# Turning an FFN's activations by 32x32 blocks and a trip through DRAM instead of TensorE transposes, with the down product one group later

## The chip, the cores and the metric

One core of a Trainium2 chip runs the whole program. The metric is the device time of one execution in microseconds. "Before" is the kernel without the change; three runs of it were timed and one execution was profiled.

## What is computed

Two blocks of a transformer, 256 tokens of width 1024, batch 1, float32 throughout. The first block has two layers, each FFN, mixer, FFN, with a gMLP mixer in the first layer and latent attention (MLA) in the second; the second block has retention and forgetting attention side by side and one more FFN. So there are five FFNs, and they are all this:

```python
def swiglu(n, w_gate, w_up, w_down):
    return (jax.nn.silu(n @ w_gate) * (n @ w_up)) @ w_down

f = swiglu(rms_norm(h, ffn_pre_g[layer, 0]), ffn_w_gate[layer, 0], ffn_w_up[layer, 0], ffn_w_down[layer, 0])
h = h + 0.5 * rms_norm(f, ffn_post_g[layer, 0])
```

The hidden width is 2816 = 11 x 256 in all five.

## The kernel before

**Tokens and weights.** The 256 tokens are two streams of 128 rows. Weights arrive from DRAM as chunks of 128x1024 floats, in the order of use, through SyncE's queue (`fetch`, line 153: the load at 158, three `raw` buffers). Each chunk is split into a rounded part `hi` (ScalarE cast, line 337) and the rest `lo` (VectorE subtract, line 338), in a ring of nine. A product of float32 accuracy is three matmuls, hi x hi, hi x lo, lo x hi (`mm3`, lines 166 to 169). A chunk costs each stream six matmuls of 512 columns. Stream 0 uses chunk s when stream 1 uses chunk s - 5, so two streams share each chunk while it is in the ring. The main loop (line 1134) takes one step a chunk; `later(st, n, fn, ...)` (line 192) runs `fn` when n + 1 more chunks of that stream are done.

**An FFN.** `ffn` (line 357) goes over 11 groups (NG) of 256 hidden columns. `up(j)` takes four chunks and makes gate and up of the group in one PSUM tile `g` of 128x512; ScalarE and VectorE make f = silu(gate) x up from it, 128 tokens by 256 columns (lines 364 to 367). The down product needs f with hidden columns on the partitions. Two chunks after, `turn(j)` (line 372) transposes the two halves of f on TensorE into PSUM, with an identity, and splits the result into `fth` and `ftl`. `down(j)` takes two chunks, 12 matmuls, and adds to the accumulator `a`. The loop at line 391 puts `down(j - 1)` after `up(j)`; the last two groups of the last FFN are held to the end:

```python
        for j in range(NG):
            yield from up(j)
            if 0 < j < NG - 2 * last:
                yield from down(j - 1)
```

`phases` (line 1211) lists the chunks in the same order, `layout` (line 1150) puts the weights into that form on the host.

**Between parts.** When a part of a stream ends, `post` (line 280) makes the next input x: ScalarE squares the accumulator, VectorE adds the two sums (line 295), GpSimd takes the power (`pow_`, line 143), VectorE makes x with it (line 299), and TensorE transposes x (line 217, `tr<-cst,x`). `prepare` (line 261) brings the gain rows `pg` and `gn` through SyncE's queue during an FFN; a small GpSimd copy into each (`touch`, line 196) sets the moment.

The order of the instructions on each engine is set by a scheduler from the program's order and its priorities; TensorE, VectorE, ScalarE, GpSimd and SyncE each work their own list in order.

Of the kernel before, what the change touches and what calls it, by code (L numbers as in the profile page):

```python
# [9 lines left out]
F32 = mybir.dt.float32  # L10
F32R = mybir.dt.float32r
# [5 lines left out]
P = 128  # L17
D = 1024
KD = D // P
FF = 2816  # L20
NG = FF // 256
# [88 lines left out]
def body(ctx: ExitStack, tc: tile.TileContext, a: dict, out: bass.AP, stop=None, dbg=None):  # L110
    nc = tc.nc
    V, S, G, PE = nc.vector, nc.scalar, nc.gpsimd, nc.tensor

    base = ctx.enter_context(tc.tile_pool(name="base", bufs=1))
    ring = ctx.enter_context(tc.tile_pool(name="ring", bufs=1))
    psg = ctx.enter_context(tc.tile_pool(name="psg", bufs=2, space=bass.MemoryType.PSUM))
    psa = ctx.enter_context(tc.tile_pool(name="psa", bufs=1, space=bass.MemoryType.PSUM))
    pst = ctx.enter_context(tc.tile_pool(name="pst", bufs=2, space=bass.MemoryType.PSUM))

    def f32(x):  # L120
        return x.bitcast(F32)
# [70 lines left out]
    def later(st, n, fn, *args):  # L192

        st.later.append([n + 1, fn, args])
# [128 lines left out]
    def acc_tile(st):  # L323
        return [psa.tile([P, 512], F32, name=f"a{st.t}{q}") for q in range(2)]

    def g_tile():
        return psg.tile([P, 512], F32, name="g")
# [8 lines left out]
    def split(hi, lo, src):  # L336
        S.copy(hi, src)  # L337
        V.tensor_tensor(lo, src, f32(hi), op=ALU.subtract)  # L338
# [6 lines left out]
    def unit(st, ps, lhs=None, nq=4, nk=2, n=512):  # L345

        for q in range(nq):
            w = yield
            k_gemm(ps, lhs or st.xt, w, nk * q, q == 0, q == nq - 1, nk, n)
# [7 lines left out]
    def ffn(st, inner={}, last=False):  # L357
        fts = {}

        def up(j):  # L360
            ps = g_tile()
            yield from unit(st, ps)
            th = base.tile([P, 256], F32, name="th", tag="th", bufs=2)
            S.activation(th, ps[:, :256], AF.Tanh, scale=st.ch)  # L364
            V.scalar_tensor_tensor(th, th, 1.0, ps[:, :256], op0=ALU.add, op1=ALU.mult)  # L365
            f = base.tile([P, 256], F32, name="f", tag="f", bufs=2)
            V.scalar_tensor_tensor(f, th, st.cc, ps[:, 256:], op0=ALU.mult, op1=ALU.mult)  # L367
            fts[j] = f
            st.mark = f[:, 0:1]
            later(st, 2, turn, j)  # L370

        def turn(j):
            f = fts[j]
            tr = pst.tile([P, 4, P], F32, name="tr")
            for k in range(2):
                PE.transpose(tr[:, k, :], f[:, k * P:(k + 1) * P], ident)  # L376
            pool, n = (enter("last"), 6) if last and j > 5 else (base, 3)
            hi = pool.tile([P, 2, P], F32R, name="fth", tag="fth", bufs=n)
            lo = pool.tile([P, 2, P], F32R, name="ftl", tag="ftl", bufs=n)
            split(hi, lo, tr[:, :2, :])  # L380
            fts[j] = hi, lo

        def down(j):
            if j == 0:
                st.acc = acc_tile(st)
            for k in range(2):
                w = yield
                f = fts[j]
                rows_gemm(st.acc, f, w, k, j + k == 0, j == NG - 1 and k == 1)

        for j in range(NG):
            yield from up(j)
            if 0 < j < NG - 2 * last:
                yield from down(j - 1)
            if callable(inner.get(j)):
                inner[j]()
            elif j in inner:
                yield from inner[j]
        for j in range(NG - 1 - 2 * last, NG):
            yield from down(j)  # L400


    def gmlp(st, pool):
# [352 lines left out]
    def block2(st, pool):  # L756
# [168 lines left out]
        ps = yield from next_unit()  # L925
        vr = pool.tile([P, 512], F32, name="vr", tag="vr", bufs=1)
        S.activation(vr, ps, AF.Copy, scale=st.c)
        orr = pool.tile([P, 512], F32, name="orr", tag="orr", bufs=2)
        sT = pool.tile([P, 4, P], F32, name="sT", tag="sT", bufs=1)

        def retain():
# [68 lines left out]
        for q in range(2):  # L1000
            tr = transposes(st, m[q], 0)
# [5 lines left out]
        with urgent():  # L1007
            for q in range(2):
                c = slice(512 * q, 512 * q + 512)
# [5 lines left out]
    def enter(name):  # L1015
        if name not in pools:
            pools[name] = [tc.alloc_tile_pool(name=name, bufs=1), 0]
        return pools[name][0]
# [92 lines left out]
    n = len(chunks)  # L1111
# [38 lines left out]
def layout(i):  # L1150

    c = np.ascontiguousarray
    o = {}

    def cols(w, unit, nk=2):

        k, n = w.shape
        return c(w.reshape(k // (P * nk), nk, P, n // unit, unit).transpose(3, 0, 2, 1, 4)).reshape(-1, P, nk * unit)

    def rowsw(w):  # L1160

        return w.reshape(-1, P, w.shape[1])

    def gu(g, u):
        both = np.stack([g.reshape(D, NG, 256), u.reshape(D, NG, 256)], 2).reshape(D, NG * 512)
        return cols(both, 512)

    fl = [(i["ffn_w_gate"][l, k], i["ffn_w_up"][l, k], i["ffn_w_down"][l, k]) for l in range(2) for k in range(2)]
    fl.append((i["w_gate_2"][0], i["w_up_2"][0], i["w_down_2"][0]))
    for n, (g, u, d) in enumerate(fl):  # L1170
        o[f"gu{n}"] = gu(g, u)
        o[f"dn{n}"] = rowsw(d)
    o["win"] = cols(i["gmlp_w_in"][0], 512)
    o["wgo"] = rowsw(i["gmlp_w_out"][0])
    o["wdq"] = cols(i["mla_w_dq"][0], 512)
    o["wdkv"] = cols(i["w_dkv"], 320)
    uq = i["mla_w_uq"][0].reshape(512, NH, 192)
    o["wuqr"] = cols(c(uq[:, :, P:]).reshape(512, 512), 512)
    o["wuq"] = cols(c(uq[:, [0, 2, 4, 6, 1, 3, 5, 7], :P]).reshape(512, 1024), 512)
    ukv = i["w_ukv"].reshape(256, NH, 256)  # L1180
    o["wukv"] = np.concatenate([cols(c(ukv[:, :, k * P:(k + 1) * P]).reshape(256, 1024), 512) for k in range(2)])
    wo = i["mla_w_o"][0].reshape(NH, P, D)
    o["wo"] = c(wo[[0, 2, 4, 6, 1, 3, 5, 7]])
    w2 = i["w_in_2"][0]
    big = np.concatenate([w2[:, 1536:2048], w2[:, 2048:2560], w2[:, 2560:3072], w2[:, 0:512], w2[:, 512:1024],
                          w2[:, 1024:1536], w2[:, 3080:4104], w2[:, 4104:5128]], 1)
    o["w2"] = cols(big, 512)
    o["w2f"] = c(w2[:, 3072:3080].reshape(8, P, 8).transpose(1, 0, 2)).reshape(P, 64)
    o["wro"] = rowsw(i["w_ret_o_2"][0])
    o["wfo"] = rowsw(i["w_fox_o_2"][0])  # L1190
    o["wout"] = rowsw(i["w_out_2"][0])
    gl = [i["ffn_pre_g"][0, 0], i["ffn_pre_g"][0, 1], i["ffn_pre_g"][1, 0], i["ffn_pre_g"][1, 1], i["mix_pre_g"][0],
          i["mix_pre_g"][1], i["kv_norm_g"], i["kv_a_norm_g"], i["mla_q_norm_g"][0], i["g_mix_2"][0], i["g_ffn_2"][0], i["g_ret_norm_2"][0],
          np.concatenate([i["g_fox_q_2"][0]] * 2), np.concatenate([i["g_fox_k_2"][0]] * 2)]
    o["pre"] = np.stack([gl[k] for k in (4, 1, 2, 5, 3, 9)])
    o["kva"], o["qn"] = i["kv_a_norm_g"].reshape(1, 256), i["mla_q_norm_g"].reshape(1, 512)
    o["gains"] = c(np.concatenate([g.reshape(-1, P).T for g in gl], 1))
    o["ffn_post_g"] = c(i["ffn_post_g"].reshape(4, D))
    o["mix_post_g"] = c(i["mix_post_g"])
    o["gmlp_ln_g"] = c(i["gmlp_ln_g"])  # L1200
    o["gmlp_ln_b"] = c(i["gmlp_ln_b"])
    o["b_forget_2"] = c(i["b_forget_2"])
    o["ws"] = c(i["gmlp_w_s"][0].transpose(2, 0, 1)).reshape(P, 16 * P)
    o["bs"] = c(i["gmlp_b_s"][0].T)
    o["x"] = c(i["x"][0])
    o["positions"] = c(i["positions"].reshape(2, P).T)
    o["c1"], o["c2"] = constants()
    return o


def phases(aps):
    def ch(name, idx):
        w = aps[name]
        return w[idx], w.shape[-1]

    def run(name, first, n):
        return [ch(name, k) for k in range(first, first + n)]

    def ffn(n, inner={}, last=False):
        r = []  # L1220
        for j in range(NG):
            r += run(f"gu{n}", 4 * j, 4)
            if 0 < j < NG - 2 * last:
                r += run(f"dn{n}", 2 * j - 2, 2)
            r += inner.get(j, [])
        return r + run(f"dn{n}", 2 * (NG - 1 - 2 * last), 2 + 4 * last)

    gm = run("win", 16, 16)
    for j in range(4):
        gm += run("win", 4 * j, 4)  # L1230
        if j:
            gm += run("wgo", 4 * j - 4, 4)
    gm += run("wgo", 12, 4)
    ml = run("wdq", 0, 4) + run("wukv", 0, 4) + run("wuqr", 0, 2) + run("wuq", 0, 4) + run("wo", 0, 8)
    b2 = run("w2", 0, 24)
    b2 += run("w2", 24, 8) + run("wro", 0, 4)
    b2 += run("w2", 32, 8) + run("wfo", 0, 4)
    b2 += run("wout", 0, 8)
    return [ffn(0), gm, ffn(1), ffn(2, {2: run("wdkv", 0, 4)}), ml, ffn(3), b2, ffn(4, last=True)]
# [18 lines left out]
```

## Time and profile before

| | |
|---|---|
| median of 3 runs | 1398.04 us (1396.69 to 1398.93) |
| the profiled execution | 1396.79 us, of which 1394.9 us are the trace's span |
| TensorE busy, matmuls | 1376.0 us, 99% |
| VectorE busy | 957.0 us, 69% |
| ScalarE busy | 717.2 us, 51% |
| GpSimd busy | 59.7 us, 4% |
| DMA engines, mean busy share of the main queue | 57.7%, 182 GB/s |

Matmuls are pipelined and their ends are modelled, so 99% says that TensorE is hardly ever without a matmul, not that it is at its peak. The weight loads of TensorE (81%) overlap the matmuls. Rows of the trace give the line of the kernel, the tile written and the tiles read, and in brackets the idle time before with what ended it.

### The profile page before, as it was taken

What the parts mean: (1) busy time and instruction counts of PE and PEld (TensorE: products, weight loads), DVE (VectorE), ACT (ScalarE), POOL (GpSimd) and SP (SyncE); (2) the same over time, 40 slices, a digit from 0 to 9 for tenths busy, and PEclk for the clock granted to TensorE, in tenths of its full rate; (3) what the DMA queues carried; (4) which work ended last, traced back from release to release, by engine and by line L of the source; (5) the groups of instructions that cost most, each with busy time, mean ns of one, the idle gap of its engine ahead of it and who ended that gap; (6) DMA issues with size and microseconds to landing.
All of it is one profiled execution on the core that took longest, in us unless ns stands there. A gap on an engine that the chain in (4) does not pass through costs nothing.

```text
span 1394.9 us, 17750 instructions
## 1 busy us (share of the span) xinstructions
PE 1376.0 (99%) x6402; PEld 1125.1 (81%) x6402; DVE 957.0 (69%) x1530; ACT 717.2 (51%) x1043; POOL 59.7 (4%) x81
## 2 busy tenths in 40 slices
PE   8999999999999999999999999999999999999998
PEld 5888887887788887888877888888878788888887
DVE  7775579977757558775569676665677865765554
ACT  6644456555544445544456655444567544544442
POOL 0000020000000001000001010000020000000000
PEclk9999999999999999999999999999999999999999
DMA  7666667554566664666655336666544355565662
GB/s 250 201 220 185 188 250 222 157 191 151 181 191 217 186 192 143 201 220 195 188 190 179 124 130 183 202 201 191 199 137 150 119 168 183 171 190 185 192 185 88
DMA packets 71656, 254.45 MB, mean 182 GB/s; under 512 B 8592, under 2 KB 10000, under 8 KB 71184
## 3 DMA queue, kind: packets, MB, share of 16 engines
q1 hardware_dynamic: 70992, 252.78, 57.7%
q8 instruction: 51, 0.84, 0.2%
q10 hardware_dynamic: 576, 0.52, 0.1%
q14 instruction: 37, 0.30, 0.1%
HBM read 252.23 MB, written 1.05 MB: 182 GB/s over the span
## 4 chain that ended last, share of the span: by engine, by line
PE 87%; DVE 6%; ACT 2%; DMA 2%; issue 1%; POOL 1%; SPq 0%; DVEq 0%; ACTq 0%; POOLq 0%
PE g L167 16%; PE g L168 16%; PE g L169 16%; PE a L169 11%; PE a L167 11%; PE a L168 11%; DVE lo L338 2%; PE tr L376 2%; PE tr L217 2%; DMA raw<-in_win 1%; POOL sm L145 1%; ACT hi L337 1%; DMA raw<-in_gu 1%; PE tr L459 0%; PE tr L722 0%
## 5 line engine op out<-in xcount | busy, mean ns | idle before, releaser
L338 DVE TENSOR_TENSOR lo<-raw,hi 128x1024 fp32r<-128x1024 f32 (+2 forms) x462 | 560.8, 1216 | 307.2 <-ACT hi L337 305.6
L337 ACT CAST hi<-raw 128x1024 fp32r<-128x1024 f32 (+2 forms) x462 | 481.2, 1044 | 428.8 <-PE g L169 205.7
L167 PE MATMUL g<-hi,xth 128*128 128x512 f32 x1040 | 414.3, 398 | 2.2 <-ACT hi L337 1.8
L168 PE MATMUL g<-lo,xth 128*128 128x512 f32 x1040 | 407.6, 392 | 2.0 <-DVE lo L338 2.0
L169 PE MATMUL g<-hi,xtl 128*128 128x512 f32 x1040 | 406.3, 391 | 0.0
L167 PEld LDWEIGHTS g<-hi,xth 128*128 128x128 f32 x1040 | 195.4, 188 | 43.0 <-ACT hi L337 3.5
L169 PEld LDWEIGHTS g<-hi,xtl 128*128 128x128 f32 x1040 | 195.4, 188 | 41.3 <-DVE sm L255 0.2
L168 PEld LDWEIGHTS g<-lo,xth 128*128 128x128 f32 x1040 | 195.6, 188 | 41.0 <-DVE lo L338 3.7
L167 PE MATMUL a<-hi,fth 128*128 128x512 f32 x440 | 175.7, 400 | 0.0
L168 PE MATMUL a<-lo,fth 128*128 128x512 f32 x440 | 172.0, 391 | 0.0
L169 PE MATMUL a<-hi,ftl 128*128 128x512 f32 x440 | 171.9, 391 | 0.0
L169 PEld LDWEIGHTS a<-hi,ftl 128*128 128x128 f32 x440 | 82.6, 188 | 17.4
L364 ACT ACTIVATE th<-g,ch 128x256 f32<-128x256 f32 x110 | 52.3, 475 | 86.4 <-PE g L169 85.2
L168 PEld LDWEIGHTS a<-lo,fth 128*128 128x128 f32 x440 | 82.8, 188 | 15.5
L167 PEld LDWEIGHTS a<-hi,fth 128*128 128x128 f32 x440 | 82.6, 188 | 15.5
L167 PE MATMUL a<-hi,xth 128*128 128x512 f32 x232 | 94.0, 406 | 0.7 <-ACT xth L337 0.6
L168 PE MATMUL a<-lo,xth 128*128 128x512 f32 x232 | 91.0, 394 | 0.0
L169 PE MATMUL a<-hi,xtl 128*128 128x512 f32 x232 | 90.9, 395 | 0.0
L365 DVE SCALAR_TENSOR_TENSOR th<-th,g 128x256 f32<-128x256 f32 x110 | 45.9, 418 | 43.5 <-ACT th L364 43.4
L337 ACT CAST fth<-tr 128x256 fp32r<-128x256 f32 x110 | 40.5, 369 | 37.6 <-PE tr L376 37.6
L367 DVE SCALAR_TENSOR_TENSOR f<-th,cc,g 128x256 f32<-128x256 f32 x110 | 52.8, 480 | 3.5
L167 PEld LDWEIGHTS a<-hi,xth 128*128 128x128 f32 x232 | 43.6, 188 | 10.3 <-ACT xth L337 2.1
(318 smaller groups left out, 1187.0 us busy)
## 6 DMA issues: line engine op xcount, KB each, us to landing
raw<-in_gu SPq DMA_DIRECT2D x220, 512.0 KB, 3.6
raw<-in_dn SPq DMA_DIRECT2D x110, 512.0 KB, 3.9
raw<-in_w SPq DMA_DIRECT2D x40, 512.0 KB, 3.3
raw<-in_win SPq DMA_DIRECT2D x32, 512.0 KB, 4.3
raw<-in_wgo SPq DMA_DIRECT2D x16, 512.0 KB, 3.6
raw<-in_wo SPq DMA_DIRECT2D x8, 512.0 KB, 3.3
raw<-in_wout SPq DMA_DIRECT2D x8, 512.0 KB, 3.3
gn<-in_pre SPq DMA_DIRECT2D x6, 512.0 KB, 5.3
```

The lines of the kernel that those rows point to most:

```text
L145: G.tensor_tensor(o, i, hp if up else hn[:, :n], op=ALU.pow)
L167: PE.matmul(o, l[0], r[0], start=start, stop=False)
L168: PE.matmul(o, l[0], r[1], start=False, stop=False)
L169: PE.matmul(o, l[1], r[0], start=False, stop=stop_)
L217: PE.transpose(tr[:, k, :], src[:, (4 * ngroup + k) * P:(4 * ngroup + k + 1) * P], ident)
L337: S.copy(hi, src)
L338: V.tensor_tensor(lo, src, f32(hi), op=ALU.subtract)
L364: S.activation(th, ps[:, :256], AF.Tanh, scale=st.ch)
L365: V.scalar_tensor_tensor(th, th, 1.0, ps[:, :256], op0=ALU.add, op1=ALU.mult)
L367: V.scalar_tensor_tensor(f, th, st.cc, ps[:, 256:], op0=ALU.mult, op1=ALU.mult)
L376: PE.transpose(tr[:, k, :], f[:, k * P:(k + 1) * P], ident)
```

## The change

In groups 0 to 7 of the first four FFNs and 0 to 9 of the last, f no longer goes through TensorE. VectorE transposes it by 32x32 blocks into `ft`; a DMA from GpSimd's queue writes `ft` to a DRAM tile `far`; four chunks later four DMAs of the same queue read `far` back into `fr` in the order in which blocks stand in their places, with a fixed permutation of the hidden columns that is made good in the rows of the down weights (`layout`). One chunk later `fr` is split into `fth` and `ftl` as `tr` was. The other groups are turned as before. `fr` has one buffer for both streams; `ft` shares the two buffers of `th`. `down(j)` follows `up(j + 2)` instead of `up(j + 1)`, and the FFN's last products are gathered at its end as the table `downs` says. To make room, one tile of the second block (`orr`) has one buffer in place of two.

```diff
-            later(st, 2, turn, j)
+            if j > (9 if last else 7):
+                later(st, 2, turn, j)
+                return
+
+            ft = base.tile([P, 256], F32, name="ft", tag="th", bufs=2)
+            V.transpose(ft, f)
+            far = dram.tile([4, 32, 4, 64], F32, name="far", bufs=6)
+            nc.gpsimd.dma_start(far.rearrange("a i c r -> (a i) (c r)"), ft)
+            later(st, 4, back, j, far)
+
+        def back(j, far):
+            fr = base.tile([P, 4, 64], F32, name="fr", bufs=1)
+            for c in range(4):
+                nc.gpsimd.dma_start(fr[32 * c:32 * c + 32], far[:, :, c, :].rearrange("a i r -> i a r"))
+            later(st, 1, parts, j, fr.rearrange("p a (k i) -> p k a i", k=2))
...
+        def parts(j, fr):
+            f = fts[j] = f_tiles(j)
+            split(*(x.rearrange("p k (a i) -> p k a i", a=4) for x in f), fr)
...
             yield from up(j)
-            if 0 < j < NG - 2 * last:
-                yield from down(j - 1)
+            for k in downs(j, last):
+                yield from down(k)
...
-        orr = pool.tile([P, 512], F32, name="orr", tag="orr", bufs=2)
+        orr = pool.tile([P, 512], F32, name="orr", tag="orr", bufs=1)
...
+        k = 10 if n == 4 else 8
+        d = d.reshape(NG, 4, 2, 32, D)
+        o[f"dn{n}"] = np.concatenate([d[:k].transpose(0, 2, 1, 3, 4).reshape(-1, P, D), d[k:].reshape(-1, P, D)])
...
+def downs(j, last):
+
+    if last:
+        return [j - 2] if 2 <= j < 9 else [7, 8, 9, 10] if j == 10 else []
+    return {0: [], 1: [], 9: [7, 8], 10: [9, 10]}.get(j, [j - 2])
```

How it moves instructions is best seen in three places. The first is TensorE in the first FFN, where the down products of the two streams meet (`a` are the accumulators, `g` the up products, `tr` the transposed f, `cst` the identity). Before:

```order
L167 MATMUL a_456<-hi,fth 128x512
L168 MATMUL a_456<-lo,fth 128x512
L169 MATMUL a_456<-hi,ftl 128x512
L376 MATMUL tr<-cst,f 128x128 x2
L167 MATMUL a_331<-hi,fth 128x512
L168 MATMUL a_331<-lo,fth 128x512
L169 MATMUL a_331<-hi,ftl 128x512
L167 MATMUL a_332<-hi,fth 128x512
L168 MATMUL a_332<-lo,fth 128x512
L169 MATMUL a_332<-hi,ftl 128x512
L376 MATMUL tr<-cst,f 128x128 x2
L167 MATMUL g<-hi,xth_225 128x512
```

The two pairs of transposes, one for each stream's f, stand among the matmuls of the weights in every group; with the change they stand there only in groups 8 to 10 (group 10 in the last FFN), and nothing takes their place.

The second is GpSimd in the middle of an FFN, where before it had no instruction at all (`far` is the DRAM tile, `fr` the tile read back; the brackets name what an instruction waits for: DMASW the landing of DMAs of GpSimd's queue, DVE VectorE). With the change:

```order
L378 DMA far<-ft 128x256 [waits DVE_49] x2
L384 DMA fr<-far 32x4x64 [waits DMASW2_49,DMASW3_49,DMASW1_49,DMASW7_49,DMASW0_49,DVE_49]
L384 DMA fr<-far 32x4x64 x3
L384 DMA fr<-far 32x4x64 [waits DMASW5_49,DMASW6_49,DMASW4_49,DMASW7_49,DMASW0_49,DVE_49]
L384 DMA fr<-far 32x4x64 x3
L378 DMA far<-ft 128x256 [waits DVE_49] x2
```

Two writes, one for each stream, are followed by four reads for one stream and four for the other; each four wait for the landing of their write and of the earlier reads into `fr`, and for VectorE to have split what `fr` held.

The third is GpSimd at the change from gMLP to the second FFN (FFN 1; the first is FFN 0) and from MLA to FFN 3, where stream 1's power `sm<-sm,hp` stands. Before, at gMLP to FFN 1 (`kr` is a tile of a later part that is cleared):

```order
L595 MEMSET kr 64x256 x2
L145 TENSOR_TENSOR sm<-sm,hp 128x1
L145 TENSOR_TENSOR c<-w,hn 128x1
L198 COPY pg<-f 128x1
L198 COPY gn<-f 128x1
```

With the change, the same place:

```order
L378 DMA far<-ft 128x256 [waits DVE_49]
L613 MEMSET kr 64x256 [waits DMAHW0_49,DMAHW1_49,PE_49,Activation_49]
L613 MEMSET kr 64x256 [waits Pool_49]
L384 DMA fr<-far 32x4x64 [waits DMASW6_49,DMASW5_49,DMASW7_49,DMASW4_49,DMASW0_49]
L146 TENSOR_TENSOR sm<-sm,hp 128x1 [waits DVE_49,Pool_49]
L384 DMA fr<-far 32x4x64 x3
L146 TENSOR_TENSOR c<-w,hn 128x1 [waits DVE_49]
```

And from MLA to FFN 3 with the change:

```order
L378 DMA far<-ft 128x256 [waits DVE_49]
L384 DMA fr<-far 32x4x64 [waits DMASW6_49,DMASW5_49,DMASW7_49,DMASW4_49,DMASW0_49]
L384 DMA fr<-far 32x4x64
L146 TENSOR_TENSOR sm<-sm,hp 128x1 [waits DVE_49]
L384 DMA fr<-far 32x4x64 x2
L146 TENSOR_TENSOR c<-w,hn 128x1 [waits DVE_49]
```

A write of stream 0's first group and one or two of its reads, which wait for the write to land, now stand ahead of stream 1's power. From FFN 1 to FFN 2 only the write stands ahead of it.

## Rows read from the trace of the kernel before

**Rows 1.** The page: busy time of each engine, and the chain that ended last.
```profile
PE 1376.0 (99%) x6402; PEld 1125.1 (81%) x6402; DVE 957.0 (69%) x1530; ACT 717.2 (51%) x1043; POOL 59.7 (4%) x81
...
PE 87%; DVE 6%; ACT 2%; DMA 2%; issue 1%; POOL 1%; SPq 0%; DVEq 0%; ACTq 0%; POOLq 0%
PE g L167 16%; PE g L168 16%; PE g L169 16%; PE a L169 11%; PE a L167 11%; PE a L168 11%; DVE lo L338 2%; PE tr L376 2%; PE tr L217 2%; DMA raw<-in_win 1%; POOL sm L145 1%; ACT hi L337 1%; DMA raw<-in_gu 1%; PE tr L459 0%; PE tr L722 0%
```
**Rows 2.** Windows, the first FFN: busy us by engine (PE to POOL), granted clock, DMA share, GB/s.
```profile
110.50:127.36 16.86, 16.86 (x77) 13.86 (x76) 9.73 (x12) 7.75 (x11) 0.00 (x0) 1.00 0.60 188
...
144.22:161.08 16.86, 16.86 (x77) 13.87 (x76) 9.74 (x12) 7.74 (x11) 0.00 (x0) 1.00 0.64 188
```
**Rows 3.** Timeline of PE, no transposes; 16 matmuls between: start us, duration.
```profile
126.48 0.39 PE L167 MATMUL g<-hi,xth 128*128 128x512 f32 x1
...
130.33 0.39 PE L169 MATMUL a<-hi,ftl 128*128 128x512 f32 x1
```
**Rows 4.** Timeline of PE around a pair of transposes.
```profile
117.12 0.39 PE L169 MATMUL a<-hi,ftl 128*128 128x512 f32 x1
117.36 0.38 PE L376 MATMUL tr<-cst,f 128*128 128x128 f32 x2
...
117.81 0.40 PE L168 MATMUL g<-lo,xth 128*128 128x512 f32 x1
```
**Rows 5.** Groups by line: busy us, mean ns | idle us before, its releasers.
```profile
L337 ACT CAST hi<-raw 128x1024 fp32r<-128x1024 f32 (+2 forms) x462 | 481.2, 1044 | 428.8 <-PE g L169 205.7 <-PE a L169 158.3 <-DMA raw<-in_gu 29.1
L338 DVE TENSOR_TENSOR lo<-raw,hi 128x1024 fp32r<-128x1024 f32 (+2 forms) x462 | 560.8, 1216 | 307.2 <-ACT hi L337 305.6
L367 DVE SCALAR_TENSOR_TENSOR f<-th,cc,g 128x256 f32<-128x256 f32 x110 | 52.8, 480 | 3.5
L338 DVE TENSOR_TENSOR ftl<-tr,fth 128x256 fp32r<-128x256 f32 x110 | 42.4, 417 | 5.9 <-ACT fth L337 5.8
L376 PE MATMUL tr<-cst,f 128*128 128x128 f32 x220 | 41.9, 272 | 0.0
L337 ACT CAST fth<-tr 128x256 fp32r<-128x256 f32 x110 | 40.5, 369 | 37.6 <-PE tr L376 37.6
L273 DVE TENSOR_SCALAR pg<-pg 128x256 f32<-128x256 f32 x24 | 5.9, 288 | 7.3 <-DMA pg<-in_ffn_post_g 7.0 <-DMA pg<-in_mix_post_g 0.4
```
**Rows 6.** DMA: one issue, a queue's total, and issues with KB and median us to landing.
```profile
118.33 0.33 SPq L158 DMA_DIRECT2D raw<-in_dn  x1
...
q10 hardware_dynamic: 576, 0.52, 0.1%
...
raw<-in_gu SPq DMA_DIRECT2D x220, 512.0 KB, 3.6
...
gn<-in_pre SPq DMA_DIRECT2D x6, 512.0 KB, 5.3
...
out<-h SPq DMA_DIRECT2D x4, 128.0 KB, 1.9
...
kva<-in_kva SPq DMA_DIRECT2D x1, 128.0 KB, 3.3
```
**Rows 7.** Timeline, gMLP to FFN 1, stream 1.
```profile
353.31 0.48 DVE L367 SCALAR_TENSOR_TENSOR f<-th,cc,g 128x256 f32<-128x256 f32 x1
...
357.50 1.23 DVE L338 TENSOR_TENSOR lo<-raw,hi 128x1024 fp32r<-128x1024 f32 x1
357.58 1.55 POOL L145 TENSOR_TENSOR sm<-sm,hp 128x1 f32<-128x1 f32 x1 [1.00 <-DVE sm L295]
...
360.13 0.63 PE L217 MATMUL tr<-cst,x 128*128 128x128 f32 x4 [0.44 <-DVE x L299]
```
**Rows 8.** Timeline, MLA to FFN 3, stream 1.
```profile
828.99 0.48 DVE L367 SCALAR_TENSOR_TENSOR f<-th,cc,g 128x256 f32<-128x256 f32 x1
...
833.37 0.55 POOL L145 TENSOR_TENSOR sm<-sm,hp 128x1 f32<-128x1 f32 x1 [7.74 <-DVE sm L295]
...
835.51 0.63 PE L217 MATMUL tr<-cst,x 128*128 128x128 f32 x4
```

## What the change was expected to do

> **What bounds the kernel now.** I began with the page. TensorE is busy for 99% of the span, holds 87% of the chain that ended last, and the transposes of f at line 376 stand in that chain with 2% [rows 1]. The reader is to see that nothing but TensorE's own stream can give time here. The granted clock is 1.00, the 2.4 GHz level, in every stretch I use.
>
> Then the windows over three groups of the first FFN [rows 2]. A period, in which both streams do one up product and one down product, takes 16.86 us; VectorE works 9.73 of it, ScalarE 7.74, GpSimd nothing, the DMA engines 60 to 64%. A period holds 6 weight chunks of 12 matmuls, so 72, and two pairs of transposes.
>
> Then the timeline, to learn what a pair really costs. The page's busy figure says 272 ns a transpose, so 0.54 a pair [rows 5]; but matmuls overlap, each is "busy" for 0.39 us and the next starts 0.23 later. In a stretch without a pair, 17 spacings take 130.33 - 126.48 = 3.85 us, 0.2265 each [rows 3]. 72 of them are 16.31 us; the two pairs have the rest of the period: (16.86 - 16.31) / 2 = **0.27 us a pair**. Read directly, from 117.12 to 117.81 there are two spacings and one pair: 0.69 - 0.45 = 0.24 [rows 4].
>
> **The change part by part.**
>
> *Transposes off TensorE.* Eight groups in four FFNs and ten in the last, two streams each: (4 x 8 + 10) x 2 = 84 pairs. 84 x 0.27 = **-22.7 us**; with 0.24 it is 20.2. Nothing else is moved between two matmuls of a steady period, so this is gained whole as long as operands come in time.
>
> *VectorE.* Each turned f adds one 32x32-block transpose of 128x256. No such row exists; the nearest are 128x256 operations of 418 to 480 ns [rows 5], a lower bound being 288 (the gain scaling, also 128x256). I take 0.48. A period gets 2 x 0.48 more: 10.7 of 16.3 us. That is hidden, because lo is early: a ring slot comes free when stream 1 has left chunk i, stream 0 then starts chunk i+6, and the slot is for chunk i+9, so three chunks of 2.72 us, less cast 1.04 and subtract 1.22, leave about 5.9 us (an estimate from [rows 2, 5]). ScalarE shows it: of the 429 us that it idles ahead of these casts, 364 end on a matmul, that is on a slot coming free [rows 5]. Cost 0. The cast and subtract of f now read SBUF, not PSUM, at 0.37 and 0.42 either way; cost 0.
>
> *GpSimd's queue.* Ten DMA issues a period where there was nothing: two writes and eight reads. Before has no DMA on this queue. From below, SyncE's issue takes 0.33 us [rows 6]. From above, GpSimd's own 128x1 operation takes 0.55 alone and 1.55 when it runs beside a subtract `lo` (357.58, beside 357.50) [rows 7, 8]. I take **x = 1.0 us** an issue, the middle, as the queue has to work for each but reads no tile. What matters is the loop through the single buffer `fr`: four issues, the landing, cast and subtract, then the other stream's four. The landing I take as 2.5 us, between the 1.9 and 3.3 of the 128 KB rows [rows 6]. A half loop is 4x + 2.5 + 0.37 + 0.42 = 4x + 3.3 = 7.3 us; two are 14.6 against a period of 16.3. It fits, with the two writes issued while a landing is waited for. The down product follows two periods after, 32 us, against some 20 for write, four chunks, reads and split. Cost **0**; at 0.33 it is 0 too, at 1.55 see the first rival.
>
> Weighed against that is a rule that speaks against the change. The row is the power's 1.55 us beside `lo` against 0.55 alone [rows 7, 8]. The Trainium skill ("SBUF — State Buffer", Who interferes with whom, with its box on the "DVE blocks DMA" trap) says that GpSimd cannot write the descriptors of its DMAs while VectorE runs an operation in a two-port performance mode, and that a VectorE operation with two SBUF inputs keeps out only GpSimd operations that read SBUF. By that rule the power's stretch agrees with the row and an issue beside `lo` would not share it; the only one-input scaling in an FFN is that of the gains, 5.9 us in all [rows 5], too little to change the sum. If the block transpose counts as a two-port operation, which no row here shows, each stops the queue for its 0.48 us, 1 us a period, and the loop still fits.
>
> *DMA engines.* 1,024 packets of 256 B and 256 of 1 KB more a period. The nearest row is the queue of 576 packets: 0.1% of 16 engines' span, about 39 ns each (19 to 58 by rounding) [rows 6]. 1,280 x 39 = 50 us over 16 engines and 16.3 us is 19%: the share goes from 62 to about 81%, at 58 ns to 90%, so weight chunks land later than 3.6 us. Three raw buffers and a chunk each 2.72 us let a chunk take 8.2 us from issue to subtracted; cast and subtract need 2.3, so a landing of up to 5.9 us costs nothing. Cost 0, bounds 0 and 6: at the four places where gain rows are fetched besides, which land in 5.3 us where a chunk lands in 3.6 [rows 6], a chunk 1.5 late.
>
> *Handovers.* GpSimd also makes the one power that stands between stream 1's sum and its x. At gmlp to FFN 1 and MLA to FFN 3 the first write and its reads of stream 0 now stand ahead of it, and the reads wait for the write to land. Now f ends at 353.79 and the power starts at 357.58, held by VectorE; TensorE waits 0.44 for the x made with it [rows 7]. Then: f 353.79, transpose to 354.4, write issued 355.4, landed 357.9, one read issued 358.9, and only then the power: 1.3 us later. At MLA to FFN 3 f ends 829.47, so the read is out at 834.6, and a second one at 835.6, where the power started at 833.37: 2.2 later; there TensorE waits for nothing now, and starts on x at 835.51 [rows 8]. With less other work queued ahead of x than before I add 1 us each: 1.3 + 2.2 + 2 = 5.5, bounds 1 (all covered) and 9. FFN 1 to FFN 2 has only a write ahead of the power: 0.
>
> *Preparing the gains.* The small copies that let SyncE fetch the next gain rows now stand behind four reads. When the queue is in time they wait little; where they wait, the weight loads behind them on SyncE's queue wait too, which the 5.9 us mostly cover. Four such places at 0.4: 1.5 us, bounds 0 and 6.
>
> *One buffer less in the retention part, down products two groups late.* The same products in another order, 0.
>
> **Sum**: -22.7 + 5.5 + 1.5 = -15.7 us. The profiled execution, 1396.8 us, becomes 1381.1; the median of the runs shown is 1.2 above it, so **1382 us**.
>
> **The rivals.**
>
> 1. *GpSimd's issues become the bound (slower).* If an issue takes 1.55 us, as the power does beside `lo`, two half loops take 2 x (4 x 1.55 + 3.3) = 19.0 us, 2.7 more than a period. Over eight periods that is 21.6 us behind; ScalarE and VectorE wait in order for the reads, and the weights' 5.9 us lead is used up first, so about 15.7 us an FFN, 78 for five (the last has ten), less 15.7: +62, **1460 us**. Even with no gain or loss: (15.7 / 5 + 5.9) / 8 = 1.13 us a period, 8x + 6.6 = 17.4, so it decides at **x = 1.36**. For it: VectorE works `lo` 45% of a period, and a small GpSimd operation was stretched threefold beside it. Against: DMA issue reads no tile. Chance 0.22, of which the part just above 1.36 gives 1400 to 1420.
>
>  The page named above gives this rival a mechanism, and by its rule for which operations lock, `lo` would not bring it about.
>
> 2. *The handovers and the weight loads take the gain back (no change).* Handovers at 9, gains at 6, late chunks at 6 more leave -2 us: **1396 us**. For it: reads that wait for a landing stand ahead of two powers, and the DMA share rises. Against: TensorE's waits there are under 1 us each today. Chance 0.06.
>
> 3. *All of it is hidden.* Other work of the last stream covers the power, and the whole 22.7 to 23.3 is kept: **1375 us**. For it: at MLA to FFN 3 TensorE did not wait at all. Chance 0.12.
>
> That the change does not do what it says is no rival: the transposes of 84 turns are gone from TensorE's order.
>
> **How the numbers follow.** The forecast, with its bounds 1376 to 1390, has 0.60. About 0.2%, 2.8 us, can be told from no change. Faster: 0.60 + 0.12 = 0.72; same: 0.06; slower: 0.22. Range: from 1374, all hidden at 0.277 a pair, to 1420, which takes in the near part of the first rival and leaves out its full size, some 0.14.
>
> **What would show it.** Right: windows over three groups of 16.3 us with 72 matmuls at 0.227 spacing; GpSimd busy or issuing 10 us a period; `fr` landing 2 to 3 us after its issue; TensorE's waits only at gmlp to FFN 1 and MLA to FFN 3, 1 to 3 us each. Wrong: periods over 16.9 us that grow within an FFN, the cast of f waiting for reads and TensorE for `hi` or `lo` behind it; chunks landing later than 5.9 us; a transpose on VectorE much over 0.5 us.

## The result and the profile after

The changed kernel took 1406.66 us in the median of 4 runs (1404.62 to 1409.01) where the kernel before took 1397.37 beside it: a ratio of 1.0066 (95% interval 1.0047 to 1.0085). It is slower by 9 us, where 15.7 us less were forecast; the time lies inside the stated range and on the other side of no change. The profiled execution took 1404.62 us, of which the span is 1402.5: the fastest of the four, so what its trace shows is rather less than the median's loss.

The page, busy time and DMA queues (q1 carries the weights, q0 is the new traffic of GpSimd's queue):

```profile
PE 1363.4 (97%) x6234; PEld 1110.0 (79%) x6234; DVE 981.2 (70%) x1614; ACT 710.9 (51%) x1041; POOL 293.1 (21%) x501
...
q1 hardware_dynamic: 70992, 252.78, 57.9%
q0 software_dynamic: 14784, 22.05, 5.5%
```

The 168 transposes are gone from TensorE (x6402 to x6234, [rows 1]); it has idle time in their place. The new traffic is 5.5% of the DMA engines' time over the whole span. The 19% that was estimated is of a period and is compared below, in the windows.

The windows of one period, once in the first FFN and twice in the last (columns as in [rows 2]):

```profile
121.50:137.80 16.30, 16.30 (x73) 13.48 (x72) 10.22 (x14) 7.79 (x11) 5.64 (x11) 1.00 0.79 227
...
1310.20:1326.50 16.30, 15.31 (x68) 12.36 (x66) 7.64 (x12) 6.08 (x9) 4.94 (x9) 1.00 0.70 211
...
1342.80:1359.10 16.30, 14.01 (x61) 10.98 (x60) 10.27 (x14) 7.35 (x10) 5.23 (x10) 1.00 0.67 217
```

In the first, TensorE is never idle and a period takes 16.3 us instead of 16.86: the gain is there. In the last FFN TensorE does 1 to 2.3 us less of work in the same time. The DMA engines are busy for 67 to 79%, where it was 60 to 64% [rows 2]; the forecast was about 81%. A period holds 14784 / 42 = 352 packets of the new queue, not 1,280, so that forecast came near by luck.

Where the time went is seen when the start of the same matmul is compared in the two traces, counting matmuls of weights alone. After minus before, by stretch of the program (us, from one profile each; three of the kernels tried below beside it):

| stretch | after | e12 | e3 | e7 |
|---|---|---|---|---|
| to the 144th matmul (start of FFN 0) | +3.4 | +2.2 | +1.0 | +2.3 |
| rest of FFN 0 | -1.0 | -0.7 | -3.6 | -3.5 |
| gMLP | 0.0 | -0.1 | -0.5 | -0.4 |
| first 12 chunks of FFN 1 | +0.7 | +0.3 | +0.6 | +0.3 |
| rest of FFN 1 | -0.2 | -2.0 | -3.3 | -3.2 |
| first 24 chunks of FFN 2 | **+7.4** | +2.7 | +3.1 | +0.4 |
| rest of FFN 2 | -3.4 | -2.4 | -3.4 | -2.4 |
| MLA, first 12 chunks of FFN 3 | +1.4 | +0.8 | +0.7 | +0.9 |
| rest of FFN 3 | -3.6 | -3.8 | -3.8 | -3.8 |
| second block to its FFN | 0.0 | 0.0 | 0.0 | 0.0 |
| last FFN | **+2.3** | -4.9 | -5.0 | -5.1 |
| sum | +6.9 | -7.9 | -14.3 | -14.5 |

So the periods do give back half a microsecond each, and it is lost again where FFN 2 starts, where FFN 0 starts, and late in an FFN. The first row is the least certain: e3 and e7 are the same kernel up to there and differ by 1.3 us. What TensorE waits for (total us, times, longest):

```profile
PE g L168 <- DVE f L368: 11.3, 13, 2.2
PE tr L218 <- DVE x L300: 5.3, 7, 1.7
```

The first row is new. An up product waits for a PSUM tile that VectorE's f of an earlier group still has to empty. The second was 3.7 us in 5 waits before.

Why f is late is seen in the timeline, all engines, in the last FFN; a `fth<-fr` is ScalarE's cast of what came back from DRAM:

```profile
1318.69 0.41 ACT L338 CAST fth<-fr 128x256 fp32r<-128x256 f32 x1 [4.26 <-DMA fr<-far]
...
1319.85 2.17 POOL L384 DMA_DIRECT2D fr<-far  x4 [6.26 <-DVE ftl L339]
...
1325.21 0.41 ACT L338 CAST fth<-fr 128x256 fp32r<-128x256 f32 x1 [3.84 <-DMA fr<-far]
1325.52 0.47 ACT L365 ACTIVATE th<-g,ch 128x256 f32<-128x256 f32 x1
...
1326.02 0.42 DVE L366 SCALAR_TENSOR_TENSOR th<-th,g 128x256 f32<-128x256 f32 x1
1326.48 0.48 DVE L368 SCALAR_TENSOR_TENSOR f<-th,cc,g 128x256 f32<-128x256 f32 x1
...
1327.11 0.47 PE L168 MATMUL g<-hi,xth 128*128 128x512 f32 x1 [1.60 <-DVE f L368]
```

ScalarE stands still for 4.26 us and casts stream 1's tile; only when VectorE has split it too may the four reads of stream 0 go into the one `fr`; ScalarE stands still again for 3.84 us, and the `th` of a group whose up product is long done is queued **behind that cast**. f follows, and TensorE has waited 1.60 us for it. The groups of those rows (busy us, mean ns | idle before):

```profile
L384 POOL DMA_DIRECT2D fr<-far x336 | 183.4, 552 | 319.5 <-DVE ftl L339 196.7 <-DMA far<-ft 33.1 <-DVE lo L339 26.8
L378 POOL DMA_DIRECT2D far<-ft x84 | 47.6, 566 | 153.6 <-DVE ft L376 121.6 <-issue 8.6 <-DVE th L366 6.8
L376 DVE STREAM_TRANSPOSE ft<-f 128x256 f32<-128x256 f32 x84 | 37.0, 440 | 0.9 <-DMA far<-ft 0.7
L338 ACT CAST fth<-fr 128x256 fp32r<-128x256 f32 x84 | 34.2, 407 | 180.0 <-DMA fr<-far 164.4 <-PE a L169 7.2 <-issue 5.2
```

ScalarE waits 164 us for reads, 84 times 2.0, where the same cast waited 38 us for TensorE before [rows 5]. An issue takes 0.55 us, a block transpose 0.44. And the landings (KB each, median us):

```profile
raw<-in_gu SPq DMA_DIRECT2D x220, 512.0 KB, 4.3
raw<-in_dn SPq DMA_DIRECT2D x110, 512.0 KB, 4.6
...
far<-ft POOLq DMA_DIRECT2D x84, 128.0 KB, 4.2
fr<-far POOLq DMA_DIRECT2D x336, 32.0 KB, 3.7
```

The round through DRAM, GpSimd's timeline in the middle of the first FFN:

```profile
126.80 2.17 POOL L384 DMA_DIRECT2D fr<-far  x4 [5.15 <-DVE ftl L339]
130.90 0.56 POOL L378 DMA_DIRECT2D far<-ft  x1 [1.92 <-DVE ft L376]
133.21 0.56 POOL L378 DMA_DIRECT2D far<-ft  x1 [1.75 <-DVE ft L376]
135.44 2.20 POOL L384 DMA_DIRECT2D fr<-far  x4 [1.68 <-DVE lo L339]
143.30 2.17 POOL L384 DMA_DIRECT2D fr<-far  x4 [5.66 <-DVE ftl L339]
```

From reads to reads it is 135.44 - 126.80 = 8.64 and 143.30 - 135.44 = 7.86: **16.5 us** against a period of 16.3. The queue itself is idle for most of it. The two halves end on different things. The reads of 143.30, stream 0's, wait for the split of stream 1's tile, which ends at 143.00. The reads of 135.44, stream 1's, do not wait for the buffer: the tile in `fr` was split by 133.22. The row names a `lo` of VectorE because that ended last by the profile, but the write that they read back, issued at 130.90, landed at 134.80. Over the whole trace 41 of the 84 groups of reads go out right after the landing of their own write, 42 right after the split of the other stream's tile.

### The profile page after: what moved, and what is told of

Read it like the earlier page. It is cut to its first block, busy times and chain, and to the rows that moved or that the text cites. A ratio compares the mean times of both kernels' runs of the same rounds, so it can differ in the third digit from the quotient of the medians.

```text
span 1402.5 us, 18583 instructions
## 1 busy us (share of the span) xinstructions
PE 1363.4 (97%) x6234; PEld 1110.0 (79%) x6234; DVE 981.2 (70%) x1614; ACT 710.9 (51%) x1041; POOL 293.1 (21%) x501
## 3 DMA queue, kind: packets, MB, share of 16 engines
q0 software_dynamic: 14784, 22.05, 5.5%
## 5 line engine op out<-in xcount | busy, mean ns | idle before, releaser
L339 DVE TENSOR_TENSOR lo<-raw,hi 128x1024 fp32r<-128x1024 f32 (+1 forms) x462 | 560.1, 1215 | 226.5 <-ACT hi L338 225.3
L338 ACT CAST hi<-raw 128x1024 fp32r<-128x1024 f32 (+1 forms) x462 | 481.1, 1044 | 322.1 <-PE g L170 94.6
L168 PE MATMUL g<-hi,xth 128*128 128x512 f32 x1040 | 412.2, 397 | 16.5 <-DVE f L368 11.3
L384 POOL DMA_DIRECT2D fr<-far x336 | 183.4, 552 | 319.5 <-DVE ftl L339 196.7
L168 PE MATMUL a<-hi,fth 128*128 128x512 f32 x440 | 172.3, 392 | 0.0
L338 ACT CAST fth<-fr 128x256 fp32r<-128x256 f32 x84 | 34.2, 407 | 180.0 <-DMA fr<-far 164.4
L339 DVE TENSOR_TENSOR ftl<-fr,fth 128x256 fp32r<-128x256 f32 x84 | 35.3, 420 | 80.2 <-ACT fth L338 80.1
L378 POOL DMA_DIRECT2D far<-ft x84 | 47.6, 566 | 153.6 <-DVE ft L376 121.6
```

The costliest lines, as they stand in the source:

```text
L168: PE.matmul(o, l[0], r[0], start=start, stop=False)
L378: nc.gpsimd.dma_start(far.rearrange("a i c r -> (a i) (c r)"), ft)
L384: nc.gpsimd.dma_start(fr[32 * c:32 * c + 32], far[:, :, c, :].rearrange("a i r -> i a r"))
```

## The experiments

Theories at the start. *Order*: stream 1's round from write, landing, reads, landing, cast, next th, f, transpose to the next write closes through ScalarE's list and takes as long as a period. *Buffer*: the two half loops through the one `fr` bind. *Load*: the DMA traffic and GpSimd's queue make the weights late. Summary, medians beside the kernel before. Every edit lets the scheduler order the engines' lists anew, so no row differs from another by its name alone:

| kernel | us | ratio (95%) | ScalarE waits for reads, us |
|---|---|---|---|
| after | 1406.7 | 1.0066 (1.0047 to 1.0085) | 164 |
| e1 two buffers | 1415.1 | 1.0114 (1.0086 to 1.0141) | 144 |
| e12 two buffers, GpSimd's order kept | 1391.3 | 0.9966 (0.9953 to 0.9978) | 107 |
| e10 four writes, one read | 1391.3 | 0.9965 (0.9953 to 0.9976) | 86 |
| e2 cast pinned | 1393.8 | 0.9981 (0.9971 to 0.9991) | 66 |
| e9 cast pinned, two buffers | 1389.6 | 0.9950 (0.9933 to 0.9966) | 18 |
| e3 cast pinned, a chunk later, two buffers | 1384.4 | 0.9911 (0.9896 to 0.9925) | 3 |
| e13 as e3, one read | 1383.9 | 0.9911 (0.9896 to 0.9925) | 2 |

**e1, two buffers.**

```diff
-            fr = base.tile([P, 4, 64], F32, name="fr", bufs=1)
+            fr = base.tile([P, 4, 64], F32, name="fr", bufs=2)
```

> Only change against the changed kernel: fr has two buffers. Order theory (the loop write, landing, read, landing, ScalarE's cast, and behind it in ScalarE's list the next th, f, block transpose and write takes as long as a period, 16.3 to 16.5 us, so that no lateness is ever caught up): 1403 to 1408 us, since the reads of stream 1 already wait for the write and not for the buffer. Buffer theory (the two half loops through the one fr bind): 1390 or less, ScalarE's 164 us of waiting for reads under 80. Load theory (22 MB more DMA and a busy GpSimd queue make the weight chunks late): 1404 to 1408.

Measured 1415.07 us (1408.23 to 1420.23), worse than every theory had it (the profile is of the slowest run). The edit changed more than a buffer: the scheduler moved stream 1's first read ahead of stream 0's write. GpSimd's timeline of e1:

```profile
118.00 0.56 POOL L384 DMA_DIRECT2D fr<-far  x1 [4.02 <-DMA far<-ft]
118.55 0.56 POOL L378 DMA_DIRECT2D far<-ft  x1
119.10 1.64 POOL L384 DMA_DIRECT2D fr<-far  x3
```

Stream 0's block transpose had begun at 115.00; its write stood behind a read that waited 4.02 us for stream 1's write to land, and went out at 118.55. In the changed kernel that gap is 0.7. So e1 tells nothing of the buffer; e12 was meant to.

**e12, two buffers with GpSimd's order kept**, the reads pinned in program order so that both writes stay ahead of them:

```diff
-                nc.gpsimd.dma_start(fr[32 * c:32 * c + 32], far[:, :, c, :].rearrange("a i r -> i a r"))
+                tc.keep_in_program_order(nc.gpsimd.dma_start(fr[32 * c:32 * c + 32], far[:, :, c, :].rearrange("a i r -> i a r")))
```

> As e1_two_fr, with the reads of fr pinned in GpSimd's queue so that both writes stand ahead of them as in the changed kernel. ScalarE's and GpSimd's orders are then those of the changed kernel and the second buffer is the only difference. Order theory (stream 1's loop from write to write, 16.3 to 16.5 us in the changed kernel, 16.8 to 16.9 in e1, 16.0 in e10): the loop is as in the changed kernel, 1400 to 1408 us. Buffer theory: 1390 or less.

Measured 1391.26 us (1389.34 to 1393.69): 15 us better than the changed kernel, near the buffer theory's bound and far from the order theory's. But the second buffer is not the only difference, as it was meant to be. The traces show that ScalarE's list changed as well: in the last FFN three casts of stream 0 stand ahead of two `th` where the changed kernel has them between the two (compare 1325.21 above). In e12:

```profile
1308.42 0.41 ACT L338 CAST fth<-fr 128x256 fp32r<-128x256 f32 x1 [1.91 <-DMA fr<-far]
1308.73 0.47 ACT L365 ACTIVATE th<-g,ch 128x256 f32<-128x256 f32 x1
...
1310.27 0.47 ACT L365 ACTIVATE th<-g,ch 128x256 f32<-128x256 f32 x1
```

Of the 14.8 us between the two profiles 4.7 stand at the start of FFN 2 and 7.2 in the last FFN, both places where ScalarE's lists differ. In five long stretches the lists of ScalarE and VectorE are the same in both (83 to 203 us of the changed kernel's trace, 407 to 540, 590 to 740, 890 to 1050, 1267 to 1318). There e12 is better by -0.3, 1.8, 0.9, 0.3 and 0.0 us, 2.7 in all. In the first of them e10 (below), with the same two lists, is better by 2.5. So the buffer with the new order is worth 15 us, and what is shown of the buffer by itself is small.

**e2, the cast pinned, one buffer.** The cast of `fr` is kept behind what the program has traced ahead of it on ScalarE, which is the next `th` of its stream:

```diff
-            split(*(x.rearrange("p k (a i) -> p k a i", a=4) for x in f), fr)
+            hi, lo = (x.rearrange("p k (a i) -> p k a i", a=4) for x in f)
+            tc.keep_in_program_order(S.copy(hi, fr))
+            V.tensor_tensor(lo, fr, f32(hi), op=ALU.subtract)
```

> Only change against the changed kernel: ScalarE's cast of fr is pinned behind what stands ahead of it in the program, so behind the same stream's next th. Order theory: 1382 to 1394 us, TensorE's 11.3 us of waiting for f under 4. Buffer theory: 1404 or more, as the buffer is held longer. Load theory: 1404 to 1408.

Measured 1393.75 us (1391.35 to 1397.67): 13 better, with the buffer still single, so the buffer is not needed for that much: the order counts. TensorE still waited 6.8 us for f, more than expected (in a profile 3 us above the median).

**e3, both, the cast one more chunk later** (`later(st, 2, parts, ...)`).

> Both: two buffers of fr, the cast pinned and one chunk later. Order theory: 1380 to 1388 us, ScalarE's wait for reads under 30 us of 164. Buffer theory: 1390 or less. Load theory: 1404 to 1408 with weight chunks still landing in 4.3 to 4.6 us.

Measured 1384.42 us (1383.04 to 1385.82), as the order theory had it; the buffer theory allowed it. Its window and its group of casts:

```profile
121.50:137.80 16.30, 16.30 (x74) 13.49 (x73) 10.31 (x15) 7.74 (x11) 5.48 (x10) 1.00 0.74 226
```

```profile
L394 ACT CAST fth<-fr 128x256 fp32r<-128x256 f32 x84 | 33.6, 403 | 45.6 <-PE a L169 39.0 <-DMA fr<-far 2.9 <-DVE h L1116 2.4
```

The wait for reads is 2.9 us in all; what is left is a wait for the split tiles of an earlier group (39.0), which are three. The load theory falls here: the traffic is the same, the chunks land in 4.3 to 4.4 us, and the kernel is 12.6 us faster than before.

**e9, both, without the extra chunk.**

> As e3_order_two_fr, but the cast pinned without the extra chunk, so right behind the same stream's next th, as in e2; against e2 it has the second buffer alone. If the place of the cast does most (order theory): 1384 to 1389 us, the rest of e2's waiting for reads (66 us) being the one buffer. If the extra chunk was what e3 gained over e2: 1391 to 1395.

Measured 1389.56 us (1388.44 to 1391.06): 4 us under e2, and e3 is 5 lower still. It lies between the two expectations, in neither.

**e10, four writes and one read**: DRAM holds the blocks in the order in which they are read.

```diff
-            nc.gpsimd.dma_start(far.rearrange("a i c r -> (a i) (c r)"), ft)
+            for b in range(4):
+                nc.gpsimd.dma_start(far[:, :, b, :].rearrange("c i r -> i c r"), ft[32 * b:32 * b + 32].rearrange("p (c r) -> p c r", c=4))
...
-            for c in range(4):
-                nc.gpsimd.dma_start(fr[32 * c:32 * c + 32], far[:, :, c, :].rearrange("a i r -> i a r"))
+            nc.gpsimd.dma_start(fr, far.rearrange("c i a r -> (c i) a r"))
```

> Only change against the changed kernel: DRAM holds the blocks in read order, so that four DMAs write and one reads. Buffer theory: each half loop is shorter by three issues of 0.55, 1.65 us: 1392 or less. Order theory: the loop through ScalarE's list has the three issues ahead of the write's landing instead of behind it and is as long as before: 1402 to 1412 us.

Measured 1391.25 us (1390.17 to 1396.16), where the buffer theory had it. What stands between the buffer's release, or the write's landing, and the next cast is shorter by three issues, and the one read of 1 KB rows landed in 3.3 us against 3.7 for each of four of 256 B (in e13 and e3, below and above, both take 4.0):

```profile
far<-ft POOLq DMA_DIRECT2D x336, 32.0 KB, 3.8
fr<-far POOLq DMA_DIRECT2D x84, 128.0 KB, 3.3
```

**e13, e3 with one read.**

> As e3_order_two_fr, with four writes and one read as in e10. Order theory: with the loop open the shorter landing of the one read gives nothing, 1382 to 1386 us (e3: 1384.4). If the DMAs' time bounds on its own: 1380 or less, by a good part of the 15 us that the one read gave in e10.

Measured 1383.88 us (1381.95 to 1385.04), the same as e3: once the cast does not hold up `th`, how fast the tile comes back no longer matters.

So the two theories were no rivals. What took the gain is ScalarE's wait for the reads ahead of `th`; its length is made of the buffer's release or the landing of the write, four issues and a landing, and it hurts because of the place of the cast. Shortening the round (e10) or moving the cast (e2) gives 15 and 13 us back; moving it with a second buffer gives 17 (e9), and with a chunk more 22 (e3). How much of the last two is the buffer's stays open, as the lists changed with it. In the last FFN the spacing of stream 1's writes shows it, five periods from the first row to the last. After:

```profile
1290.44 0.56 POOL L378 DMA_DIRECT2D far<-ft  x1 [1.93 <-DVE ft L376]
...
1376.07 0.56 POOL L378 DMA_DIRECT2D far<-ft  x1 [1.45 <-DVE ft L376]
```

In e2:

```profile
1286.38 0.56 POOL L378 DMA_DIRECT2D far<-ft  x1
...
1367.98 0.56 POOL L378 DMA_DIRECT2D far<-ft  x1
```

85.63 / 5 = 17.13 us against 81.60 / 5 = 16.32, which is 72 matmuls at 0.2267: e2 is paced by TensorE, the changed kernel by its round through DRAM.

**e6, e3 with the reads pinned behind the power** on GpSimd's queue (the edit of e12).

> As e3_order_two_fr, with the reads of far pinned behind what stands ahead of them in the program on GpSimd's queue, so behind stream 1's power. If the power's place behind the reads costs what the prediction said at gMLP to FFN 1 and MLA to FFN 3 (1.3 and 2.2 us and 1 each): 1379 to 1382 us against e3's 1384.4. If it is less cover alone: 1383 to 1386.

Measured 1384.28 us (1383.70 to 1385.18), e3's time. At gMLP to FFN 1, VectorE's sum and GpSimd in e3:

```profile
354.08 0.27 DVE L296 TENSOR_SCALAR sm<-sm 128x1 f32<-128x1 f32 x1
...
355.20 0.56 POOL L384 DMA_DIRECT2D fr<-far  x1 [1.69 <-DMA far<-ft]
355.82 0.56 POOL L146 TENSOR_TENSOR sm<-sm,hp 128x1 f32<-128x1 f32 x1
```

and in e6:

```profile
354.63 0.27 DVE L296 TENSOR_SCALAR sm<-sm 128x1 f32<-128x1 f32 x1
...
355.05 1.57 POOL L146 TENSOR_TENSOR sm<-sm,hp 128x1 f32<-128x1 f32 x1 [1.00 <-DVE sm L296]
```

The two traces stand 0.55 us apart here, so times are counted from the start of the sum. With the read ahead of it the power starts 1.74 us after it instead of 0.42, the 1.3 us later that were forecast, but ends only 0.3 later, 2.30 against 1.99: in e6 it runs beside the subtract and is stretched [rows 7], in e3 it is not.

**e7, e3 with groups 0 and 1 of FFN 2 as in the kernel before** (`downs` gives [], [0], [1], [] for the first four groups there, and the weights' rows of these two groups keep their order).

> As e3_order_two_fr, but in FFN 2 groups 0 and 1 are turned on TensorE and their down products follow one group on, as in the kernel before. If the missing down products at the start of FFN 2, beside the latent's products, cost the 5 us that stand there in every kernel with the late down product: 5 saved, 4 pairs of transposes given back at 0.27, so 1379 to 1382 us. If something else costs there (the power, the writes): 1384 to 1387.

Measured 1382.90 us (1382.59 to 1383.40), 0.9901 of before (0.9886 to 0.9916): the fastest here. In the table above the start of FFN 2 goes from +3.1 to +0.4 for 1.0 given back in the rest of it. What the edit takes away at that start costs some 3 us in e3, not 5, and the time lies between the two expectations. The edit takes away the late down product and the first groups' trip through DRAM together. For the down product speaks that e4, which has no DMA path at all, loses 5.2 us at the same start.

**e4 and e5, the late down product alone**: all groups turned on TensorE; in e5 the 84 turns four chunks later.

```diff
-            if j > (9 if last else 7):
+            if True:
```

> All groups are turned on TensorE as before, the down product follows two groups on and orr has one buffer: the rest of the change without the DMA path. Order, buffer and load theories: 1395 to 1400 us, as before (1397.4). If the late down product itself costs (up products back to back at an FFN's start with two PSUM tiles): 1402 or more.

> As e4_late_down_only, but f of those 84 turns is transposed four chunks later, at the chunk after which the changed kernel splits, so that the three split buffers are held no longer than there. If those buffers made up e4's loss away from the handovers (1.4 to 2.1 us at each of four transposes): 1399 to 1404 us, with 4 to 7 us lost from FFN 1 to FFN 2 alone. If the late down product costs everywhere: 1407 or more. If it costs nothing: 1397.

Measured 1408.71 us (1408.45 to 1409.12) and 1409.29 (1408.79 to 1410.14): dear, but not a clean price. In e4 the three split tiles are held longer than in the changed kernel, and transposes wait for them:

```profile
PE tr L399 <- DVE ftl L339: 5.4, 4, 1.7
```

In e5 the scheduler put the turns right ahead of their down products, and TensorE stood 3.8 us for one cast in FFN 0. At the start of FFN 2 they lose 5.2 and 1.6 us; of e5's loss some 8 us stand before the 144th matmul. What the late down product costs by itself elsewhere stays open.

**e8, the write from SyncE's queue.**

> As e3_order_two_fr, with the write of far issued from SyncE's queue. Read for the landing of the write, 4.1 us from GpSimd's queue: under 3 us if the queue makes it slow (GpSimd's own part), 3.5 or more if it is the load of the DMA engines. The time: 1384 to 1400 us, as the weight loads stand behind the write.

Measured 1387.49 us (1386.33 to 1388.65). The landing is what it was, so it is not GpSimd's queue that makes it long. The 3 us more than e3 stand at the start of FFN 2, +7.0 against +3.1:

```profile
far<-ft SPq DMA_DIRECT2D x84, 128.0 KB, 4.1
```

**e11, e7 with groups 8 and 9 as well.**

> As e7_early_down_ffn2, with groups 8 and 9 of the first four FFNs by VectorE and DRAM too: 16 pairs more off TensorE. If nothing else comes into the way: 16 x 0.27 = 4.3 less than e7's 1382.9, 1377 to 1380 us. If the last groups' reads come late for the FFN's last products or stand ahead of the next part's power: 1382 to 1388.

Measured 1394.71 us (1386.11 to 1399.89, widely spread). That is above both expectations. In the trace, which is of a run of 1388.87, each of the first four FFNs takes 2 to 3 us more behind its start than in e7, 6 us of which are left at the end of the kernel. The next part's x comes late (in e7 4.4 us in 6 waits):

```profile
PE tr L218 <- DVE x L300: 8.9, 8, 1.8
```

In these four FFNs the last three groups are better left on TensorE; what the slower runs lose besides was not profiled.

## Why the prediction was wrong, step by step

**Transposes off TensorE, -22.7 us: right.** Periods fell from 16.86 to 16.3 us; where nothing else is lost (e3, the stretches behind each FFN's start) 19 us were gained of the 22.7. The other transposes stand in the starts, where losses cover them.

**VectorE, 0.48 us a transpose, hidden: right.** 0.44. The cast of f took 0.41 instead of 0.37, the subtract 0.42 as assumed.

**GpSimd's queue: the step that failed.** "A half loop is 4x + 2.5 + 0.37 + 0.42 = 4x + 3.3 = 7.3 us; two are 14.6 against a period of 16.3. It fits [...] Cost 0." The term mis-sized is the landing: 2.5 was taken, between a row of an output written at the kernel's end (1.9) and one of a gain row (3.3) [rows 6]; measured are 4.2 for the write and 3.7 for a read (3.2 to 4.5 us from the last of four issues to the cast in the stretches shown). The issue was taken too long, 1.0 for 0.55, which hid part of it. A term put at nothing is the landing of the write ("with the two writes issued while a landing is waited for"): stream 1's reads stood behind it for 2.2 us after `fr` was free, from 133.22 to 135.44. So two halves are 16.5 us and not 14.6. The step also asked only whether the loop keeps up on the average. It did not ask where the cast stands in ScalarE's list: ahead of `th` and of weight casts, each of which then waits for a landing. That wait, with the loop long by 0.2 us a period in the first FFN and 0.8 in the last, took 22 us (1406.7 to e3's 1384.4, in which the cast, the buffer and the lists differ).

That the load makes the landing long is seen in the trace of the changed kernel itself. The last four reads go out when the weights are all in: the DMA engines are 14% busy, and the same 32 KB from the same queue land in 1.9 to 2.0 us. The window, and the view of these four by tile:

```profile
1381.00:1385.00 4.00, 4.00 (x19) 3.30 (x18) 2.64 (x4) 0.80 (x2) 2.15 (x4) 1.00 0.14 33
```

```profile
DMA to landing us min/median/max: 1.9/2.0/2.0
```

Of all its reads, the 58 with the weights' queue under 40% busy in the 4 us after the issue landed in 2.0 us (median), the 186 with 60% and more in 4.2. The Trainium skill ("DMA: Bandwidth & Descriptors", Anatomy of one DMA) gives a DMA of this queue about 2.0 us plus its bytes at 436 GB/s; an estimate from that is 2.1 us for a read and 2.3 for a write. The trace agrees where the engines are nearly idle; under the weights' load the rows have 3.7 and 4.2, and they decide.

**The first rival** had the right place, ScalarE waiting in order for the reads, and the wrong price: not an issue of 1.36 us or more, but a landing. Of the signs of being wrong, the cast waiting for reads came true; TensorE then waited for f, not for `hi` or `lo`. The chance of 0.22 for slower stood on the stretch beside `lo`, which never touched an issue: four in a row take 2.17 to 2.21 us, one group 2.29. The rule of the Trainium skill ("SBUF — State Buffer", Who interferes with whom), that a two-input VectorE operation keeps out only GpSimd operations that read SBUF, agrees with that: the power is stretched to 1.57 us, the issue is not. Neither is it by the block transposes: 13 reads issued beside one took 0.55 to 0.56 us.

**DMA engines, 0: right in the end.** 22 MB more make chunks land in 4.3 to 4.6 us instead of 3.6 to 3.9, under the 5.9 that were allowed; e3, with the same traffic, shows no cost of it.

**Handovers, 5.5: wrong in cause, and near in size by luck.** In the changed kernel the starts of FFN 0, 1, 2 and 3 lose 3.4, 0.7, 7.4 and 1.4 us, in e3 1.0, 0.6, 3.1 and 0.7: 12.9 and 5.4. The two places that were to cost 2.3 and 3.2 us cost 0.7 and 1.4 at the most, and the power behind the reads costs nothing that can be told in the time (e6). The largest is FFN 1 to FFN 2, which the prediction put at 0. In the changed kernel some 1.4 of the 7.4 us are the clock's: TensorE stood for 2.17 us, and soon after its granted clock was 0.50, the 1.2 GHz level, for about 3 us, with seven spacings of 0.427 us instead of 0.227. In e3 it stands for 2.13 us at the same place and the clock stays at 1.00, so the stand by itself does not explain it.

```profile
562.18 0.47 PE L168 MATMUL g<-hi,xth 128*128 128x512 f32 x1 [2.17 <-DVE f L368]
```

```profile
562.80:565.80 3.00, 3.00 (x8) 2.34 (x7) 3.00 (x6) 1.51 (x3) 0.60 (x1) 0.50 0.57 186
```

**Preparing the gains, 1.5: nothing.** SyncE waits 20.8 us for the small copies into the gain rows, where it waited 21.6 before.

**Down products two groups late, 0: wrong** at the start of FFN 2, as far as e4 and e7 show; elsewhere its price stays open.

## What to carry to other kernels

When work is moved into a round trip through memory, it is not enough that its bandwidth and its mean rate fit: look up in the order which instruction first waits for the landing, and what stands behind it in that engine's list. Here the scheduler had put the one cast too far forward; pinning it behind the next group's work and a chunk later, with a second buffer, turned +0.7% into -0.9%. A landing under load is to be taken from rows that stand beside the same load. And where a scheduler orders the lists, an edit of one line changes more than that line: compare the lists before a difference is put down to the edit.

## Not expected of the hardware

A DMA issue on GpSimd's queue took 0.55 us, the same beside VectorE's subtracts and block transposes, where a 128x1 operation of GpSimd goes from 0.56 to 1.57 us. A 128 KB write of a tile to DRAM landed in 4.1 to 4.2 us from either queue while weights streamed. A 32 KB read landed in 2.0 us without the weights and in 3.7, the median of all, among them.
